# A hybrid encoder layer: the attention loop by pairs of steps

## The chip, the cores and the metric

The kernel runs on one core of one Trainium2 chip. The metric is the time of one execution on the device in microseconds; the median of three runs counts. The core has five engines with a queue each, which run side by side and wait for each other by semaphores: TensorE (PE; its weight loads are shown apart as PEld), VectorE (DVE), ScalarE (ACT), GpSimd (POOL) and SyncE (SP, which issues most transfers). On each of them instructions start in the order in which the program lists them.

## The reference

One layer of a Hymba-style encoder: 2048 positions, width 1024, float32. A normed input is projected once; its columns feed an attention branch (MLA, 4 heads) and a state-space branch (S5, 32 groups of channels, forward and backward); both are normed, gated, concatenated, projected and added to the input.

```python
h = _rms_norm(x, pre_norm_g[l]);  z = h @ w_in[l]
z_q, z_kv, z_kr, g_attn, u_ssm, g_ssm = jnp.split(z, split_points, axis=-1)
...
def attend_block(args):                         # 128 queries, all 4 heads, all 2048 keys
    qn, qr = args
    s = (jnp.einsum('bqhd,bkhd->bhqk', qn, k_nope, preferred_element_type=jnp.float32)
         + jnp.einsum('bqhr,bkr->bhqk', qr, k_rope, preferred_element_type=jnp.float32))
    p = jax.nn.softmax(s * scale, axis=-1).astype(v.dtype)
    return jnp.einsum('bhqk,bkhd->bqhd', p, v)
...
ssm = _s5_bidirectional(u_ssm, ...)             # two associative scans over the positions
ssm = jax.nn.gelu(ssm);  ssm = ssm * jax.nn.sigmoid(ssm @ w_glu[l] + b_glu[l])
mixed = jnp.concatenate([attn, ssm], axis=-1) @ w_out[l]
x = x + _rms_norm(mixed, post_norm_g[l])
```

## The kernel before

Three phases. Phase 1 (to about 390 us) computes `z` in tiles of 128 positions. Phase 3 (from about 1200 us) gates both branches and multiplies by `w_out`. The change lies in phase 2 between them: one loop in which attention and S5 are interleaved by hand. No scheduler reorders it (`manual_schedule`): each engine gets its instructions in the order in which the code emits them, and a wait is put wherever an instruction needs another engine's result or a buffer that is still in use.

Products are made in float32r with operands split in a high and a low part (`hi + lo`). A **unit** is one head of one block of 256 queries (two query tiles of 128); there are 32 units (`NU`), of 8 **steps** each, 256 steps in all. Step `t` of unit `n` does the following (`i = t % 8`):

- `scores` (L1098): five matmuls of 128 queries against 512 keys into the PSUM tile `sc` (pool `psS`, 2 buffers), then on VectorE `nm`, the row maximum of these 512 scores (L1108).
- `transp` (L1145): four transposes by TensorE, of an older step's normed exponentials, into the PSUM tile `pt` (pool `psP`, 2 buffers). ScalarE copies it to `phi`, the high part (L1159); VectorE later makes `plo`, the low part, as `pt - phi` (L1573). Both lie in pool `pp`, 2 buffers each.
- `expo` (L1111): ScalarE makes `e = exp(sc - max)` with its row sum (L1114).
- `stats` (L1118), once per unit: VectorE and ScalarE work out the factors `f` that bring the four blocks of a row to one maximum and divide by the sum; `norm` (L1135) multiplies an `e` by its factor, on ScalarE (L1143) for most of the loop, on VectorE (L1139) in its last 23 steps.
- `av` (L1163): six matmuls of `phi` and `plo` with the keys' compressed values into `av`. After the eighth of a unit ScalarE copies it to `avs` (L1176), and `unit_out` multiplies by the head's value weights (`po`).

The lags, in steps behind the scores: `norm` 9 (`NLAG`), `transp` 11 (`LAG`), `av` 12 (`LAG + AVLAG`). So TensorE's order in a step is five matmuls of scores, four transposes, six of `av` for the transposes of the step before.

Between these stand the steps of S5 (`s5_pre`, `s5_post`): a group of channels starts every 7 steps (`START`; two of them 6 steps apart) and takes 15. On VectorE a group needs `ta`, `tb` (L996, L997), `X` (L1001), four scans (L1008, L1009), `hc` twice (L1017, L1021) and a split `wTl` (L196), nearly all in `s5_pre`, ahead of a step's `nm`. GpSimd makes `tb2` (L1018) and the tables of the next groups (L971, L972, L975). The queries of the next block (`qprep`: matmuls, copies L730 and L761, and on VectorE L732, L746, L764) are made a piece per step at a step's end. In the last 23 steps `out_weights` prepares the weights of phase 3 in the same place, with a copy on ScalarE (L1228) in each step.

Of the kernel before, what the change touches and what calls it, by code (L numbers as in the profile page):

```python
# [147 lines left out]
def tile_hymba(ctx, tc, x, pos, inv_freq, pre_g, w_in, q_g, w_uqT, w_uqr, kv_g, w_ukT, w_uv, attn_g,  # L148
# [202 lines left out]
    def s5_params():  # L351
# [37 lines left out]
        # F = (lam_bar - 1) / lam  # L389
# [17 lines left out]
        # powers of lam_bar, 0 .. T, in the order of each direction  # L407
# [29 lines left out]
        # phasors of chunk 32 i + 2 j + a: ph32 * (0..7) (+ phi), for a = 0, 1, and ph2 * (0..15)  # L437
# [13 lines left out]
        for nm, src in (("b", ph2), ("a", ph32)):  # L451
# [21 lines left out]
            # the backward direction turns the other way  # L473
# [11 lines left out]
        # B_bar = F B; B'' = B_bar e^{-i phi}; C' = lam_bar C  # L485
# [3 lines left out]
        def cm(orr, oi, ar, ai, xr_, xi_):  # L489
            """(orr, oi) = (ar + i ai)(xr + i xi), a over the last dimension."""  # L490
# [32 lines left out]
        # centre lag: Re(C B_bar) of both directions + D  # L523
        # (eight groups at a time: theirs are the blocks on the diagonal)
# [36 lines left out]
    def step():  # L561
        """A slice of the tables, of about BUDGET elements."""
# [15 lines left out]
    # absorbed weights: W_uq[h] W_uk[h]^T  # L578
# [23 lines left out]
    # the first tile is loaded and normed by halves  # L602
# [48 lines left out]
    # ------------------------------------------------------------------ phase 2  # L651
    # (the gate columns of the last two tiles run under its start)
# [5 lines left out]
    ep = pool(ph2, "ep", 13)  # L658
# [37 lines left out]
    # queries of a block of 256: each piece's last results are split a step later  # L696
# [74 lines left out]
    def both(*gens):  # L771
        """Step some routines in turn; what each returns."""
# [14 lines left out]
    # the gate columns of the last two tiles run under the start of the attention  # L787
# [58 lines left out]
    # S5  # L846
# [8 lines left out]
    def s5_load(q):  # L855
        """The tables of four groups."""
# [34 lines left out]
    def ops4(tile_, q_r, q_i, c1, c2):  # L891
        """The operands of tile_[., 2, s, h] = q_r[s] c1[., h] + q_i[s] c2[., h]."""
# [9 lines left out]
    def two(eng, tile_, tmp, *o):  # L902
        """The two products of a table; later they are added."""
# [18 lines left out]
    def k_build(q):  # L922
        """The kernels of the lags within a chunk, and their windows for each position."""
# [755 lines left out]
```

## Time and profile before

| | us |
|---|---|
| three runs: median (lowest to highest) | 1434.57 (1433.16 to 1434.58) |
| the profiled execution: span, first to last instruction | 1431.5 |
| attention loop: first score to last score | 394.2 to 1169.2 |
| of it with S5 (steps 3 to 228) | 400.5 to 1098.1 |
| of it with the weights of phase 3 (steps 233 to 255) | 1111.3 to 1167.9 |

The page gives no time of its own for the profiled execution beside its span, which is 3.1 us below the median of the runs. Busy time of an engine is the time in which at least one of its instructions ran; on TensorE these overlap, and their ends are modelled. A row of a timeline gives start, duration, engine, line, what is written and read, and in brackets how long the engine had stood idle and what released it.

### The profile page before, as it was taken

What the parts mean: (1) busy time and instruction counts of PE and PEld (TensorE: products, weight loads), DVE (VectorE), ACT (ScalarE), POOL (GpSimd) and SP (SyncE); (2) the same over time, 40 slices, a digit from 0 to 9 for tenths busy, and PEclk for the clock granted to TensorE, in tenths of its full rate; (3) what the DMA queues carried; (4) which work ended last, traced back from release to release, by engine and by line L of the source; (5) the groups of instructions that cost most, each with busy time, mean ns of one, the idle gap of its engine ahead of it and who ended that gap; (6) DMA issues with size and microseconds to landing.
All of it is one profiled execution on the core that took longest, in us unless ns stands there. A gap on an engine that the chain in (4) does not pass through costs nothing.

```text
span 1431.5 us, 24291 instructions
## 1 busy us (share of the span) xinstructions
PE 1359.6 (95%) x9016; PEld 1221.6 (85%) x9016; DVE 1053.7 (74%) x1876; ACT 789.0 (55%) x1796; POOL 624.9 (44%) x616
## 2 busy tenths in 40 slices
PE   7999999999989999999999998999999989999998
PEld 7999999999968788887888887887888878788886
DVE  5456545332588888898989888988888895876774
ACT  6321222122457767767677676676677775544542
POOL 2102321233364655555556555645542695323340
PEclk9999999999999999999999999999999999999999
DMA  8322332442610110201102011020100345345432
GB/s 293 89 61 66 80 87 73 98 122 73 150 35 19 39 34 5 54 19 31 41 5 61 12 32 41 23 43 5 32 5 9 101 128 131 118 148 179 145 103 88
DMA packets 122133, 102.91 MB, mean 72 GB/s; under 512 B 14672, under 2 KB 107104, under 8 KB 122016
## 3 DMA queue, kind: packets, MB, share of 16 engines
q1 hardware_dynamic: 110384, 89.43, 22.3%
q0 software_dynamic: 2272, 7.62, 2.0%
q10 hardware_dynamic: 9360, 4.33, 1.5%
q8 instruction: 70, 1.15, 0.3%
q14 instruction: 47, 0.39, 0.1%
HBM read 63.80 MB, written 37.54 MB: 71 GB/s over the span
## 4 chain that ended last, share of the span: by engine, by line
PE 59%; DVE 26%; ACT 5%; issue 4%; POOL 2%; DMA 2%; SPq 1%; ACTq 0%; POOLq 0%; DVEq 0%
DVE plo L1573 5%; DVE nm L1108 4%; PE po L202 4%; PE po L203 4%; PE po L204 4%; PE pt L1151 3%; DVE hc L1017 3%; DVE G L1009 3%; DVE G L1008 3%; PE z_ga L203 2%; PE z_ga L204 2%; PE z_ga L202 2%; PE av L1173 2%; PE z_u L204 2%; PE z_u L202 2%
## 5 line engine op out<-in xcount | busy, mean ns | idle before, releaser
L1114 ACT ACTIVATE e<-sc,nm 128x512 f32<-128x512 f32 x256 | 176.4, 689 | 141.1 <-DVE nm L1108 139.8
L1573 DVE TENSOR_TENSOR plo<-pt,phi 128x512 fp32r<-128x512 f32 x255 | 175.0, 686 | 49.2 <-ACT phi L1159 46.3
L1159 ACT ACTIVATE phi<-pt 128x512 fp32r<-128x512 f32 x256 | 152.8, 597 | 72.9 <-PE pt L1151 72.4
L1108 DVE TENSOR_REDUCE nm<-sc 128x1 f32<-128x512 f32 x256 | 175.0, 683 | 17.6 <-PE sc L1107 15.6
L1173 PE MATMUL av<-plo,kn_h 128*128 128x256 f32 x512 | 150.6, 294 | 30.0 <-DVE plo L1573 29.5
L1171 PE MATMUL av<-phi,kn_h 128*128 128x256 f32 x512 | 165.7, 324 | 13.3 <-ACT avs L1176 13.2
L1143 ACT ACTIVATE e<-e,f 128x512 f32<-128x512 f32 x226 | 163.8, 725 | 1.5 <-DVE f L1132 1.5
L1151 PEld LDWEIGHTS pt<-ident,e 128*128 128x128 f32 x1024 | 127.8, 141 | 38.9 <-DVE e L1139 4.5
L1151 PE MATMUL pt<-ident,e 128*128 128x128 f32 x1024 | 154.8, 274 | 4.3 <-DVE e L1139 3.5
L1172 PE MATMUL av<-phi,kn_l 128*128 128x256 f32 x512 | 144.6, 282 | 0.0
L1173 PEld LDWEIGHTS av<-plo,kn_h 128*128 128x128 f32 x512 | 96.5, 189 | 40.1 <-DVE plo L1573 39.3
L1018 POOL TENSOR_TENSOR tb<-G,t 128x512 f32<-128x512 f32 x32 | 41.6, 1301 | 192.2 <-DVE G L1009 192.2
L1103 PE MATMUL sc<-kT_h,qo 128*128 128x512 f32 x256 | 114.7, 448 | 2.9 <-ACT e L1114 1.4
L1171 PEld LDWEIGHTS av<-phi,kn_h 128*128 128x128 f32 x512 | 97.6, 191 | 16.6 <-ACT avs L1176 16.5
L202 PE MATMUL po<-woh,ah 128*128 128x512 f32 (+1 forms) x264 | 102.6, 389 | 1.9 <-ACT u L1410 1.9
L203 PE MATMUL po<-wol,ah 128*128 128x512 f32 (+1 forms) x264 | 102.4, 388 | 0.0
L204 PE MATMUL po<-woh,al 128*128 128x512 f32 (+1 forms) x264 | 102.3, 388 | 0.0
L1104 PE MATMUL sc<-kT_l,qo 128*128 128x512 f32 x256 | 101.5, 396 | 0.0
L1106 PE MATMUL sc<-krS,qo 128*128 128x512 f32 x256 | 101.3, 396 | 0.0
L1107 PE MATMUL sc<-krS,qo 128*128 128x512 f32 x256 | 101.2, 395 | 0.0
L1105 PE MATMUL sc<-kT_h,qo 128*128 128x512 f32 x256 | 100.8, 394 | 0.0
L1172 PEld LDWEIGHTS av<-phi,kn_l 128*128 128x128 f32 x512 | 97.7, 191 | 0.0
(337 smaller groups left out, 4148.6 us busy)
## 6 DMA issues: line engine op xcount, KB each, us to landing
g_d<-gst SPq DMA_DIRECT2D x64, 128.0 KB, 2.0
g<-g_d SPq DMA_DIRECT2D x16, 512.0 KB, 5.7
xr<-in_x_dram SPq DMA_DIRECT2D x16, 512.0 KB, 6.7
xt<-in_x_dram SPq DMA_DIRECT2D x15, 512.0 KB, 3.8
out_dram<-res SPq DMA_DIRECT2D x15, 512.0 KB, 3.1
u_d<-ust ACTq DMA_DIRECT2D x64, 64.0 KB, 2.1
u<-u_d SPq DMA_DIRECT2D x64, 64.0 KB, 2.5
o_d<-o SPq DMA_DIRECT2D x32, 128.0 KB, 1.8
```

The lines of the kernel that those rows point to most:

```text
L202: PE.matmul(ps, ahi, bhi, start=first, stop=False)
L203: PE.matmul(ps, ahi, blo, start=False, stop=False)
L204: PE.matmul(ps, alo, bhi, start=False, stop=last)
L1108: V.tensor_reduce(st["nm"][:, qt, kb:kb + 1], ps, AX.X, ALU.max, negate=True)
L1114: A.activation(e, st.pop("s"), AF.Exp, bias=st["nm"][:, qt, kb:kb + 1], accum_out=st["L"][:, qt, kb:kb + 1])
L1143: A.activation(e, e, AF.Copy, scale=f)
L1151: PE.transpose(pt[:, kk, qt, :], st["e"][qt, kt // 4][:, o:o + P], ident)
L1159: A.activation(hi, ptf, AF.Copy)
L1171: PE.matmul(o, kn_h[:, kt, :], hi[:, w], start=kt == 0, stop=False)
L1172: PE.matmul(o, kn_l[:, kt, :], hi[:, w], start=False, stop=False)
L1173: PE.matmul(o, kn_h[:, kt, :], lo[:, w], start=False, stop=kt == NT - 1)
L1573: V.tensor_tensor(lo[0], lo[1], f32(lo[2]), ALU.subtract)
```

## The change

The loop goes by pairs of steps. Pair `p` covers steps `2p` and `2p + 1`:

- `scores` makes two score tiles, of both query tiles with the same 512 keys: ten matmuls, and after each five its `nm`.
- Both `transp` of the pair follow, eight transposes in a row. They only write `pt`; the copies to `phi` and the subtractions for `plo` are now written in the loop, behind both `expo`, the first half of `stats`, the S5 steps `s5_post(2p)` and the piece `between(2p)` of the next queries or weights.
- Then `unit_out`, the first `av`, `s5_pre(2p + 1)`, the second `av`, `s5_post(2p + 1)`, `between(2p + 1)`.
- The lags become 4, 5 and 6 pairs: `norm` 8, `transp` 10, `av` 12 steps behind the scores, two steps at a time. `av` works on the transposes of the pair before.
- Pool `ep` (tiles `e`) has 12 buffers in place of 13; `pp`, `psP` and `psS` keep 2 per tag. A pair writes two `phi` and two `plo` while those of the pair before are still to be read by its `av`.
- The last unit's norms are given out at once, to V, A, V, A, G, G, G, G.

The rest is the same: the instructions and their sizes, phases 1 and 3, S5. Comments and docstrings are gone, which moves line numbers a little (`nm` L1109, `e` L1115, `norm` L1144, `transp` L1152, `av` L1170 to L1172, `phi` L1612, `plo` L1614).

```diff
-    ep = pool(ph2, "ep", 13)
+    ep = pool(ph2, "ep", 12)
...
+    def scores(qo, st, k):
+        c = slice(k * 512, (k + 1) * 512)
+        st["s"] = []
+        for qt in range(2):
+            w = slice(qt * P, (qt + 1) * P)
+            ps = psS.tile([P, 512], F32, tag="s", name="sc")
...
+            V.tensor_reduce(st["nm"][:, qt, k:k + 1], ps, AX.X, ALU.max, negate=True)
+            st["s"].append(ps)
...
-        ptf = pt.rearrange("p a b c -> p (a b c)")
-        A.activation(hi, ptf, AF.Copy)
         st["p"][j] = hi, lo
-        return lo, ptf, hi
+        return pt.rearrange("p a b c -> p (a b c)"), hi, lo
...
-    NLAG, LAG, AVLAG = 9, 11, 1
+    NLAG, LAG, AVLAG = 4, 5, 6
...
-    for t in range(8 * NU + LAG + AVLAG + 3):
...
+    for p in range(4 * NU + AVLAG + 1):
+        n, k = divmod(p, 4)
+        t = 2 * p
...
+        if not tail and p >= NLAG:
+            for i in range(2):
+                m, kk = divmod(p - NLAG, 4)
+                norm(sts[m], 2 * kk + i, "A" if state[0] is None else "V")
...
+        s5_pre(t)
...
+            scores(qo[b][h], sts[n], k)
+        m, kk = divmod(p - LAG, 4)
+        pts = [transp(sts[m], 2 * kk + i, p3) for i in range(2)] if 0 <= m < NU else []
+        if not tail:
+            for i in range(2):
+                expo(sts[n], 2 * k + i)
+            if k == 3:
+                sts[n]["stats"] = stats(sts[n])
+                run(sts[n]["stats"], 1)
+        s5_post(t)
...
+            between(t)
+        for pt_, hi_, lo_ in pts:
+            A.activation(hi_, pt_, AF.Copy)
+        for pt_, hi_, lo_ in pts:
+            V.tensor_tensor(lo_, pt_, f32(hi_), ALU.subtract)
...
+            unit_out(*units[m], sts.pop(m))
+        m, kk = divmod(p - AVLAG, 4)
+        if 0 <= m < NU:
+            av(sts[m], 2 * kk)
+        s5_pre(t + 1)
+        if 0 <= m < NU:
+            av(sts[m], 2 * kk + 1)
+        s5_post(t + 1)
...
+            between(t + 1)
```

What this does to the order on two engines, each at the same place of the program: around the four scans of one S5 group and the end of a unit, where `m` and `f` of `stats` stand. Names are those of the code; the numbers behind `pt`, `G`, `X` are buffers. ScalarE before, three steps:

```order
L1143 ACTIVATE e<-e,f 128x512
L887 ACTIVATE mh<-m_8026 128x512
L1159 ACTIVATE phi<-pt_8218 128x512
L1114 ACTIVATE e,L<-sc,nm 128x512
L1037 ACTIVATE y_2_7421<-py 128x2x128
L1143 ACTIVATE e<-e,f 128x512
L1159 ACTIVATE phi<-pt_8260 128x512
L1114 ACTIVATE e,L<-sc,nm 128x512
L1125 ACTIVATE f<-f 128x8
```

ScalarE in the changed kernel, two pairs:

```order
L1144 ACTIVATE e<-e,f 128x512 x2
L1115 ACTIVATE e,L<-sc,nm 128x512 x2
L1037 ACTIVATE y_3_8523<-py 128x2x128
L1612 ACTIVATE phi<-pt_8790 128x512
L1612 ACTIVATE phi<-pt_8797 128x512
L1181 ACTIVATE o<-po 128x256
L730 ACTIVATE qo_1_8838<-psq,kvgs 128x256
L1144 ACTIVATE e<-e,f 128x512 x2
L1115 ACTIVATE e,L<-sc,nm 128x512 x2
L1126 ACTIVATE f<-f 128x8
L1612 ACTIVATE phi<-pt_8871 128x512
L1612 ACTIVATE phi<-pt_8878 128x512
```

`phi` stood ahead of its step's `e`; now both `phi` stand behind both `e`, and behind what `s5_post`, `between` and `stats` put there (`y`, `f`). VectorE before, two steps:

```order
L1108 TENSOR_REDUCE nm<-sc 128x1
L1573 TENSOR_TENSOR plo<-pt_8218,phi 128x512
L1008 SCALAR_TENSOR_TENSOR G_4637<-tab_6803,X_4639 64x255
L1009 SCALAR_TENSOR_TENSOR G_4637<-tab_6803,X_4639 64x255
L1008 SCALAR_TENSOR_TENSOR G_4637<-tab_6803,X_4639 64x255
L1009 SCALAR_TENSOR_TENSOR G_4637<-tab_6803,X_4639 64x255
L1108 TENSOR_REDUCE nm<-sc 128x1
L1122 TENSOR_REDUCE m<-nm 128x2
L1124 TENSOR_TENSOR f<-m,nm 128x8
L1573 TENSOR_TENSOR plo<-pt_8260,phi 128x512
```

VectorE in the changed kernel, from one pair's second `plo` to the next pair's:

```order
L1614 TENSOR_TENSOR plo<-pt_8797,phi 128x512
L1008 SCALAR_TENSOR_TENSOR G_4637<-tab_6831,X_4639 64x255
L1009 SCALAR_TENSOR_TENSOR G_4637<-tab_6831,X_4639 64x255
L1008 SCALAR_TENSOR_TENSOR G_4637<-tab_6831,X_4639 64x255
L1009 SCALAR_TENSOR_TENSOR G_4637<-tab_6831,X_4639 64x255
L1017 TENSOR_TENSOR hc<-G_4637,t_8596 128x512
L1109 TENSOR_REDUCE nm<-sc 128x1 x2
L1123 TENSOR_REDUCE m<-nm 128x2
L1125 TENSOR_TENSOR f<-m,nm 128x8
L732 SCALAR_TENSOR_TENSOR qo_1_8838<-psq,kvgs,qo_1_8838 128x256
L1614 TENSOR_TENSOR plo<-pt_8871,phi 128x512
L1614 TENSOR_TENSOR plo<-pt_8878,phi 128x512
```

One `nm` and one `plo` took turns, with S5 between the steps; now two `nm` come, then what `s5_post(2p)`, `between(2p)` and `stats` have (here `m`, `f`, `qo`), two `plo`, and then the S5 work of both steps together. TensorE's order is ten matmuls of scores, eight transposes, and twelve of `av` with the S5 and query products between.

## Rows read from the trace of the kernel before

**Rows 1.** Page, part 1: busy us, share of the span, instructions.

```profile
PE 1359.6 (95%) x9016; PEld 1221.6 (85%) x9016; DVE 1053.7 (74%) x1876; ACT 789.0 (55%) x1796; POOL 624.9 (44%) x616
```

**Rows 2.** Windows: start:end, us, each engine's busy us, granted clock, DMA.

```profile
400.48:1098.09 697.61, 653.12 (x4270) 571.04 (x4269) 616.44 (x1053) 489.25 (x1150) 383.87 (x360) 1.00 0.11 26
...
1111.29:1167.93 56.64, 53.78 (x339) 46.45 (x338) 47.87 (x80) 40.76 (x94) 42.78 (x36) 1.00 0.39 110
```

**Rows 3.** Waits in 400.48 to 1098.09, by engine: us, times, longest.

```profile
PE av L1173 <- DVE plo L1573: 28.3, 32, 2.6
PE av L1171 <- ACT avs L1176: 12.8, 11, 1.8
...
DVE plo L1573 <- ACT phi L1159: 34.1, 70, 1.4
...
ACT e L1114 <- DVE nm L1108: 133.3, 109, 3.9
```

**Rows 4.** Timeline, ScalarE and VectorE in steps 103 to 105.

```profile
701.25 0.60 ACT L1159 ACTIVATE phi<-pt 128x512 fp32r<-128x512 f32 x1 [0.89 <-PE pt L1151]
...
701.88 0.69 DVE L1573 TENSOR_TENSOR plo<-pt,phi 128x512 fp32r<-128x512 f32 x1 [0.32 <-ACT phi L1159]
...
708.02 0.69 DVE L1108 TENSOR_REDUCE nm<-sc 128x1 f32<-128x512 f32 x1
...
708.75 0.69 ACT L1114 ACTIVATE e<-sc,nm 128x512 f32<-128x512 f32 x1 [0.28 <-DVE nm L1108]
...
709.43 0.71 ACT L1143 ACTIVATE e<-e,f 128x512 f32<-128x512 f32 x1
```

**Rows 5.** Timeline, TensorE: the first score matmul of two steps without S5.

```profile
1165.62 0.40 PE L1103 MATMUL sc<-kT_h,qo 128*128 128x512 f32 x1
...
1167.92 0.40 PE L1103 MATMUL sc<-kT_h,qo 128*128 128x512 f32 x1
```

**Rows 6.** Groups in 400.48 to 1098.09: count, busy us, mean ns, idle before.

```profile
L196 DVE TENSOR_TENSOR wTl<-pw,wTh 128x256 fp32r<-128x256 f32 x32 | 13.6, 425 | 15.6 <-ACT wTh L195 15.5
L732 DVE SCALAR_TENSOR_TENSOR qo<-psq,kvgs,qo 128x256 fp32r<-128x256 f32 x28 | 13.2, 473 | 0.0
...
L764 DVE TENSOR_TENSOR qo<-ptr,qo 128x128 fp32r<-128x128 f32 x56 | 12.2, 278 | 0.0
...
L1124 DVE TENSOR_TENSOR f<-m,nm 128x8 f32<-128x8 f32 x28 | 8.6, 308 | 1.0
...
L730 ACT ACTIVATE qo<-psq,kvgs 128x256 fp32r<-128x256 f32 x28 | 13.1, 469 | 3.5 <-PE psq L204 3.5
L195 ACT ACTIVATE wTh<-pw 128x256 fp32r<-128x256 f32 x32 | 12.3, 384 | 0.0
L1037 ACT ACTIVATE y<-py 128x256 f32<-128x256 f32 x31 | 11.8, 382 | 3.6 <-PE py L1034 3.6
L761 ACT ACTIVATE qo<-ptr 128x128 fp32r<-128x128 f32 x56 | 10.8, 283 | 1.6 <-PE ptr L758 1.6
...
L1125 ACT ACTIVATE f<-f 128x8 f32<-128x8 f32 x28 | 5.7, 205 | 0.2 <-DVE f L1124 0.2
```

**Rows 7.** Groups in 1111.29 to 1167.93: the weights' copy.

```profile
L1228 ACT ACTIVATE woh<-raw,ga 128x512 fp32r<-128x512 f32 x15 | 10.8, 721 | 5.3 <-DMA raw<-in_w_out_dram 5.3
```

**Rows 8.** S5's `hc`: its two groups (400.48 to 1098.09), then single ones.

```profile
L1017 DVE TENSOR_TENSOR hc<-G,t 128x512 f32<-128x512 f32 x32 | 52.3, 1635 | 0.0
...
L1021 DVE TENSOR_TENSOR hc<-hc,tb 128x512 f32<-128x512 f32 x31 | 40.7, 1311 | 2.5 <-POOL tb L1018 2.5
...
621.48 2.02 DVE L1017 TENSOR_TENSOR hc<-G,t 128x512 f32<-128x512 f32 x1
...
710.02 0.68 DVE L1017 TENSOR_TENSOR hc<-G,t 128x512 f32<-128x512 f32 x1
```

**Rows 9.** Windows around the longest wait of TensorE; the clock comes after POOL.

```profile
510.00:515.00 5.00, 2.40 (x13) 1.93 (x12) 4.78 (x10) 1.97 (x5) 4.37 (x4) 0.89 0.15 25
515.00:520.00 5.00, 4.92 (x27) 4.05 (x26) 4.75 (x9) 3.30 (x8) 2.44 (x3) 0.77 0.00 0
```

More of the change, by code (lines that the diff above doesn't have):

```diff
@@ L1545, in tile_hymba, with between @@
     p3 = None
-    TAIL = [[(0, "V"), (1, "A"), (2, "G"), (3, "G")], [(k, "G") for k in range(4, 8)]]
-    for t in range(8 * NU + LAG + AVLAG + 3):
+    TAIL = "VAVAGGGG"
+    def between(t):
         n, i = divmod(t, 8)
-        if n >= 1 and i == 0 and n - 1 < NU:
-            run(sts[n - 1]["stats"], 1)
-        if t < 8 * NU and t >= NLAG:
-            norm(sts[(t - NLAG) // 8], (t - NLAG) % 8, "A" if late is None else "V")
-        s5_pre(t)
+        late_, qb_, qn_ = state
         if n < NU:
@@ L1557, in tile_hymba @@
             b, h = units[n]
-            if i == 0:
+            if b + 1 < 8:
+                k = 8 * h + i
+                if k == 0:
+                    qb_, qn_ = qprep(b + 1, psQ, "q"), 0
+                held = qn_ % 2 == 1
+                if qb_ and (held if i == 3 else i != 4 and PLACE.get(t, (0, 0))[1] in QOFF):
+                    qn_ += 1
+                    try:
+                        next(qb_)
+                    except StopIteration as e_:
+                        qo[b + 1] = e_.value
+                        qb_ = None
@@ new lines, in between @@
+            if h == NH - 1 and i == 7:
+                assert b == 7 or b + 1 in qo
+                qo.pop(b)
+            if late_ is None and t >= START[NG] + 8 and b == 7:
+                s5x.close()
+                ph2q.close()
+                late_ = out_weights()
+        if late_ is not None:
+            next(late_, None)
+        state[:] = late_, qb_, qn_
+    state = [None, None, 0]
+    for p in range(4 * NU + AVLAG + 1):
+        n, k = divmod(p, 4)
+        t = 2 * p
+        tail = n >= NU
+        if k == 0 and n >= 1 and n - 1 < NU:
+            run(sts[n - 1]["stats"], 1)
+        if not tail and p >= NLAG:
+            for i in range(2):
+                m, kk = divmod(p - NLAG, 4)
+                norm(sts[m], 2 * kk + i, "A" if state[0] is None else "V")
+        elif p == 4 * NU:
+            for i, eng in enumerate(TAIL):
+                norm(sts[NU - 1], i, eng)
+        s5_pre(t)
+        if not tail:
+            b, h = units[n]
+            if k == 0:
@@ L1601, in tile_hymba @@
-        if n < NU and h == NH - 1 and i == 7:
-            assert b == 7 or b + 1 in qo
-            qo.pop(b)
-        if late is None and t >= START[NG] + 8 and b == 7:
-            s5x.close()
-            ph2q.close()
-            late = out_weights()
-        if late is not None:
-            next(late, None)
-        if t == 8 * NU - 1:
-            assert next(late, "end") == "end"
+        s5_post(t)
+        if tail:
+            next(p3)
+        else:
+            between(t)
+        for pt_, hi_, lo_ in pts:
+            A.activation(hi_, pt_, AF.Copy)
@@ new lines, in tile_hymba @@
+        for pt_, hi_, lo_ in pts:
+            V.tensor_tensor(lo_, pt_, f32(hi_), ALU.subtract)
+        m, kk = divmod(p - AVLAG - 1, 4)
+        if 0 <= m < NU and kk == 3:
+            unit_out(*units[m], sts.pop(m))
+        m, kk = divmod(p - AVLAG, 4)
[5 more added lines that the diff above has]
+        s5_post(t + 1)
+        if tail:
+            next(p3)
+        else:
+            between(t + 1)
@@ L1612, in tile_hymba @@
+        if p == 4 * NU - 1:
+            assert next(state[0], "end") == "end"
             ph3w.close()
```

59 lines of the change are left out of this document (8 added, 51 removed).

## The prediction

> **What bounds the kernel now.** I read the page's first part, the windows of the attention loop, the waits inside it, and then a few steps of its timeline. The page shows TensorE busy for 95% of the span [rows 1], so one looks for its waits first. The loop has to be read by itself. While S5 runs beside attention (steps 3 to 228, 697.6 us), VectorE is busy for 616.4 us, ScalarE for 489.3 and GpSimd for 383.9 [rows 2]: two engines are nearly full there. TensorE's waits are few: 28.3 us in 32 waits for `plo`, 12.8 us in 11 waits for `avs` [rows 3]. They come where S5's burst on VectorE (scans, `hc`) delays a step's `plo`, which `av` wants one step later. VectorE idles for 697.6 - 616.4 = 81.2 us, of which 34.1 us are waits for `phi` [rows 2, 3].
>
> So the loop is bound by TensorE with VectorE close behind, and the question is not only what the change takes from TensorE's 41 us of waits, but what it asks of VectorE. VectorE has a slack of 81.2 us. Of the 112.5 pairs of this stretch 109 hold transposes (the first ones come in pair 5), so that is 0.74 us for each of these.
>
> **What the change does to TensorE.** The matmuls are the same in number and size. A plain step starts 2.30 us after the one before [rows 5], a plain pair takes 4.6 us, and with S5 and queries TensorE is busy for 653.1 / 112.5 = 5.8 us a pair [rows 2]. Eight transposes in a row in place of twice four change a wait for a weight load at most; no row shows eight here, TensorE does not set the pace below, and I cost it at nothing. `av` follows its transposes by a pair, behind ten score matmuls and eight transposes, so `plo` and `avs` get about two more microseconds than in the step-wise order. The two waits of [rows 3] lose their cause: up to 41 us, if TensorE stays the bound.
>
> **What it does to ScalarE and VectorE.** This is the term that I think decides. Before, ScalarE's order in a step is `phi`, then `e`: `phi` waits only for the transposes, so VectorE can go from `nm` to `plo` almost at once. In the timeline one `plo` starts 0.04 us behind its `nm`, at 708.75 [rows 4]. In the changed order both `e` stand ahead of both `phi` on ScalarE, and on VectorE both `nm` ahead of both `plo`, with the S5 work behind them. As each engine keeps its order, every pair now runs through one chain: second `nm` (VectorE), second `e`, first `phi` (ScalarE), first `plo` (VectorE), second `plo`, S5, next pair's `nm`. From the end of the second `nm` to the start of the first `plo` VectorE can only do what the code puts between. The parts of that gap are in [rows 4]: `nm` ends at 708.71 and `e` starts at 708.75 (0.04); ScalarE takes its next instruction at 709.43 (0.68); a `phi` takes 0.60; `plo` starts at 701.88, 0.03 behind the `phi` that began at 701.25. That is 1.35 us, and it is larger than the 0.74 us of slack.
>
> What fills the gap on VectorE: `f` of `stats` always (8.6 us in all), and for even steps alone `wTl`, `qo` twice, half of (13.6 + 13.2 + 12.2) us [rows 6]. Together 28.1 us. What lengthens it on ScalarE, by standing ahead of `phi`: the exponential of `f` (5.7 us), and half of `wTh`, `y` and the two `qo` copies, half of (12.3 + 11.8 + 13.1 + 10.8) us [rows 6]. Together 29.7 us. These cancel but for 1.6 us; smaller groups of both kinds are left out.
>
> The sum for this stretch: VectorE's own work 616.4, plus 109 x 1.35 = 147.2, plus 1.6, is 765.2 us against 697.6 now: **+68 us**. TensorE's 5.8 us a pair then lies within the chain's 6.8, and the removed waits come back as waits for the chain.
>
> **The last 22 steps** (233 to 254, 11 pairs, 56.6 us with VectorE busy for 47.9 [rows 2]). Here the norms are on VectorE, and each `between` puts a copy of weights on ScalarE, 0.72 us [rows 7]; that of the even step now stands in the gap. 47.9 + 11 x (1.35 + 0.72) = 70.7 us: **+14 us**. The steps between both stretches and the loop's first steps have little VectorE work; I take them as they are. Behind the last scores the transposes and `av` go on without `e`, so the chain is absent; the norms of the last unit are spread in another way, worth some 2 us either way.
>
> **The unknown price: S5's `hc`.** Its two instructions take 1.64 and 1.31 us in the mean, single ones 0.68, others 2.02 [rows 8]; by the timeline the long ones run beside GpSimd's work on the next tables. The change moves both in time against GpSimd. All 64 short would give 32 x (0.96 + 0.63) = 51 us back, all long would cost 32 x (0.38 + 0.71) = 35 us. GpSimd's order is the same and it still starts that work when the scans end, so I take the means as they are and keep both ends for the range. [...]
>
> Sum: 1431.5 + 68 + 14 = 1513.5 us of span; the runs' median lies 3.1 us above the profiled span, so **1517 us**, 5.7% slower.
>
> **Rivals.**
>
> *The chain is covered and TensorE keeps the pace (faster).* If VectorE's forced idle time were below 0.74 us a pair, the loop would not be longer than now; below 5.8 - 616.4 / 112.5 = 0.33 us TensorE alone would set it, and its 41 us of waits would go: about 1394 us. For it speaks that these waits are plain in [rows 3] and that `av` gets a pair's time. Against it: ScalarE already waits 133.3 us for `nm` [rows 3], so `e` follows VectorE closely, and the order leaves VectorE nothing else to do. 6 in 100. That the idle time comes out near 0.74 us, as more work falls into the gap than I counted: 1435 us, 4 in 100.
>
> *TensorE's side of the pair joins the chain (slower still).* `pp` keeps two buffers, so a pair's `phi` must wait until the same pair's `av` has read the older `phi`, and `av` stands behind the transposes and what S5 and the queries put there. Two S5 groups span seven pairs; in the three of them with least S5 work on VectorE the `av` may end later than the second `e`, by up to a microsecond. 109 x 3/7 x 1.0 = 47 us: about 1564 us. For it: TensorE needs 5.8 us a pair and the chain 6.8, a small margin. Against: in the other pairs the chain is the longer by far. 7 in 100.
>
> *The clock falls.* [...] 8 in 100.
>
> **How the numbers follow.** The forecast gets 75 in 100, the rivals 6, 4, 7 and 8. The range takes in most of the `hc` ends and of the two slower rivals: 1517 - 47 = 1470 to 1562 us. About 0.2% (3 us) is what a measurement of this kernel can tell from no change; so faster 0.06, the same 0.04, slower 0.90.
>
> **What would show it.** Right: `plo` waits for `phi` on VectorE some 100 times, by 1.0 to 1.4 us each, far over 100 us in sum against 34.1 now; `av` no longer waits for `plo` or `avs`; TensorE's waits move to `pt` for `plo` and to `sc` for `e`; VectorE's busy time stays near 616 us in a stretch of about 765. Wrong: if TensorE's waits shrink and the stretch is under 697 us, the chain is covered; if TensorE shows long stretches at the lower clock, or `phi` waits for `av` rather than for its place behind `e`, one of the slower rivals holds; if `hc` moves by more than 20 us in sum, the price of [rows 8] was the mistake.

## The result, and the profile after

The changed kernel takes **1537.5 us** (median of 4 runs, 1536.4 to 1538.0) against 1434.4 us: the ratio is 1.072, 95% interval 1.0704 to 1.0735. The forecast was 1517 us in a range of 1470 to 1562: the direction and the mechanism held, the size was 20 us short. The profiled execution spans 1534.7 us against 1431.5, so 103.1 us are to be found in the trace.

Of these, 85.3 us lie in steps 3 to 228 (782.9 us against 697.6, [rows 2]), 14.5 in steps 234 to 254 (66.4 against 51.8 us), and the remaining 3.3 before, between and behind these (5.2 more from step 254 to the end, 271.1 against 265.9 us, and 2 less ahead of step 3). The windows of these two stretches in the changed kernel (start:end, us, busy us of PE, PEld, DVE, ACT and POOL, granted clock, DMA):

```profile
398.44:1181.37 782.93, 682.64 (x4279) 595.65 (x4277) 592.78 (x1056) 485.26 (x1151) 384.87 (x362) 0.96 0.11 24
1197.19:1263.56 66.37, 54.48 (x309) 44.72 (x307) 47.66 (x75) 35.35 (x83) 40.48 (x34) 0.95 0.33 91
```

VectorE was 88% busy in the S5 stretch and is now 76% busy (592.8 of 782.9 us). No engine is full: the loop is set by engines that wait for each other. The same stretch by waits (us, times, longest):

```profile
ACT e L1115 <- DVE nm L1109: 180.8, 101, 4.9
DVE plo L1614 <- ACT phi L1612: 110.3, 75, 3.2
...
PE sc L1104 <- ACT e L1115: 64.0, 35, 3.7
...
DVE plo L1614 <- PE av L1171: 30.7, 17, 3.6
DVE nm L1109 <- PE sc L1108: 18.9, 21, 3.2
DVE wTl L196 <- ACT wTh L195: 18.6, 17, 1.7
ACT phi L1612 <- PE av L1171: 11.9, 18, 1.5
...
PE ptr L758 <- ACT o L1181: 10.2, 7, 3.5
PE psq L202 <- ACT o L1181: 9.4, 5, 3.2
```

`av` no longer waits for `plo` or `avs`, whose 28.3 and 12.8 us stood first in [rows 3]. In their place TensorE waits 64.0 us for `e` ahead of its scores and 23.1 us for `o` ahead of the query products (`ptr`, `psq` and 3.5 us of `psr`), and VectorE 110.3 + 30.7 us ahead of `plo`. The groups of VectorE in that stretch (count, busy us, mean ns, idle time before them):

```profile
L1614 DVE TENSOR_TENSOR plo<-pt,phi 128x512 fp32r<-128x512 f32 x216 | 141.7, 688 | 142.6 <-ACT phi L1612 110.3 <-PE av L1171 30.7
...
L1021 DVE TENSOR_TENSOR hc<-hc,tb 128x512 f32<-128x512 f32 x31 | 39.9, 1288 | 0.6
L1017 DVE TENSOR_TENSOR hc<-G,t 128x512 f32<-128x512 f32 x31 | 30.7, 989 | 0.4
...
L196 DVE TENSOR_TENSOR wTl<-pw,wTh 128x256 fp32r<-128x256 f32 x32 | 13.4, 418 | 18.6 <-ACT wTh L195 18.6
```

`plo` and the `wTl` that lies ahead of it in even steps collect 142.6 + 18.6 = 161.2 us of idle time. The chain of waits through one such pair, in which the exponential of `f` (0.20 us) stands between `e` and `phi` (start, us, what):

```profile
716.58 0.61 DVE nm L1109
...
717.21 1.31 ACT e L1115 x3
...
718.91 0.61 ACT phi L1612
...
720.16 0.68 DVE plo L1614
```

This is the forecast chain: `nm`, `e`, `phi`, `plo` hand the work from VectorE to ScalarE and back, one after the other.

A second path was not forecast. The timeline of one place, TensorE, ScalarE and VectorE (start, us; in brackets the idle time before it and what ended that), and the window of the scores that follow:

```profile
660.00 0.38 PE L202 MATMUL psq<-zh,wab_h 128*128 128x256 f32 x1 [2.19 <-ACT o L1181]
```

```profile
658.59 1.09 ACT L1612 ACTIVATE phi<-pt 128x512 fp32r<-128x512 f32 x2
659.54 0.41 ACT L1181 ACTIVATE o<-po 128x256 f32<-128x256 f32 x1
```

```profile
662.95 0.69 DVE L1109 TENSOR_REDUCE nm<-sc 128x1 f32<-128x512 f32 x1 [2.44 <-PE sc L1108]
664.90 0.69 DVE L1109 TENSOR_REDUCE nm<-sc 128x1 f32<-128x512 f32 x1 [1.26 <-PE sc L1108]
```

```profile
661.30:664.70 3.40, 3.40 (x10) 2.53 (x9) 0.69 (x1) 2.19 (x5) 0.00 (x0) 0.53 0.02 5
```

`o`, the copy of a unit's output out of the one PSUM buffer that it shares with the query products, stands on ScalarE behind both `e` and both `phi`. The query product waits 2.19 us for it; in the 3.40 us of the window behind that wait the granted clock is 0.53 in the mean, while TensorE is busy throughout, and both `nm` of the next pair wait, 3.7 us in sum.

### The profile page after: what moved, and what is told of

The parts are those of the page before. It is cut to its first block, busy times and chain, and to the rows that moved or that the text cites. A ratio compares the mean times of both kernels' runs of the same rounds, so it can differ in the third digit from the quotient of the medians.

```text
span 1534.7 us, 24449 instructions
## 1 busy us (share of the span) xinstructions
PE 1396.6 (91%) x9016; PEld 1250.6 (81%) x9016; DVE 1033.1 (67%) x1876; ACT 783.3 (51%) x1798; POOL 620.0 (40%) x614
## 4 chain that ended last, share of the span: by engine, by line
PE 59%; DVE 22%; ACT 11%; issue 6%; DMA 2%; SPq 1%; POOL 0%; ACTq 0%; DVEq 0%; POOLq 0%
ACT e L1115 5%; DVE plo L1614 4%; PE pt L1152 3%; PE po L202 3%; PE po L203 3%; PE po L204 3%; DVE nm L1109 3%; ACT phi L1612 3%; PE sc L1104 3%; DVE G L1009 2%; DVE G L1008 2%; PE sc L1105 2%; PE sc L1106 2%; PE sc L1107 2%; PE sc L1108 2%
## 5 line engine op out<-in xcount | busy, mean ns | idle before, releaser
L1614 DVE TENSOR_TENSOR plo<-pt,phi 128x512 fp32r<-128x512 f32 x256 | 167.6, 688 | 171.8 <-ACT phi L1612 136.1
L1115 ACT ACTIVATE e<-sc,nm 128x512 f32<-128x512 f32 x256 | 173.8, 682 | 213.7 <-DVE nm L1109 213.4
L1144 ACT ACTIVATE e<-e,f 128x512 f32<-128x512 f32 x228 | 153.9, 736 | 83.8 <-DVE f L1133 83.8
L1104 PE MATMUL sc<-kT_h,qo 128*128 128x512 f32 x256 | 115.4, 451 | 78.6 <-ACT e L1115 77.0
L1109 DVE TENSOR_REDUCE nm<-sc 128x1 f32<-128x512 f32 x256 | 165.9, 682 | 20.7 <-PE sc L1108 19.4
L1170 PE MATMUL av<-phi,kn_h 128*128 128x256 f32 x512 | 158.9, 310 | 0.0
L1612 ACT ACTIVATE phi<-pt 128x512 fp32r<-128x512 f32 x256 | 142.1, 602 | 15.2 <-PE av L1171 11.9
L1152 PEld LDWEIGHTS pt<-ident,e 128*128 128x128 f32 x1024 | 121.2, 144 | 31.0 <-DVE plo L1614 15.3
L1172 PE MATMUL av<-plo,kn_h 128*128 128x256 f32 x512 | 145.4, 284 | 0.0
L1152 PE MATMUL pt<-ident,e 128*128 128x128 f32 x1024 | 139.9, 278 | 5.9 <-DVE plo L1614 5.6
L1104 PEld LDWEIGHTS sc<-kT_h,qo 128*128 128x128 f32 x256 | 51.2, 200 | 97.7 <-ACT e L1115 87.8
L1106 PE MATMUL sc<-kT_h,qo 128*128 128x512 f32 x256 | 107.0, 418 | 0.0
L1107 PE MATMUL sc<-krS,qo 128*128 128x512 f32 x256 | 107.0, 418 | 0.0
L1108 PE MATMUL sc<-krS,qo 128*128 128x512 f32 x256 | 106.0, 414 | 0.0
L1170 PEld LDWEIGHTS av<-phi,kn_h 128*128 128x128 f32 x512 | 98.7, 193 | 1.1
```

Source lines behind the costliest of these rows:

```text
L1104: PE.matmul(ps, qo[:, 0, w], kT_h[:, c], start=True, stop=False)
L1109: V.tensor_reduce(st["nm"][:, qt, k:k + 1], ps, AX.X, ALU.max, negate=True)
L1115: A.activation(e, st["s"][qt], AF.Exp, bias=st["nm"][:, qt, kb:kb + 1], accum_out=st["L"][:, qt, kb:kb + 1])
L1144: A.activation(e, e, AF.Copy, scale=f)
L1152: PE.transpose(pt[:, kk, qt, :], st["e"][qt, kt // 4][:, o:o + P], ident)
L1170: PE.matmul(o, kn_h[:, kt, :], hi[:, w], start=kt == 0, stop=False)
```

## The experiments

All compute the whole result. Stage times are from the first score matmul of step 4 to that of step 228 ("S5 stretch", one step less than in [rows 2]) and of step 234 to 254 ("late"). They come from the profiled execution, which lies within 0.3% of the median, for e10 0.7% above it. Each ratio is against runs of the kernel before that were made beside it.

| kernel | median us | ratio to before | S5 stretch | late |
|---|---|---|---|---|
| before | 1434.4 | 1 | 696.5 | 51.8 |
| changed | 1537.5 | 1.072 | 780.0 | 66.4 |
| e1 `plo` behind S5 | 1469.4 | 1.026 | 709.2 | 67.3 |
| e2 three buffers | 1525.6 | 1.065 | 770.0 | 67.8 |
| e3 `e, phi, e, phi` | 1529.9 | 1.067 | 782.4 | 59.9 |
| e4 before, `phi` behind `e` | 1611.1 | 1.124 | 859.2 | 63.4 |
| e5 norms behind | 1544.6 | 1.078 | 803.9 | 54.0 |
| e6 `phi` ahead of `e` | 1472.2 | 1.026 | 730.5 | 56.9 |
| e7 `phi`, `plo` at the end | 1557.9 | 1.087 | 800.2 | 62.3 |
| e8 before, lag of two | 1453.1 | 1.014 | 717.7 | 50.9 |
| e9 e1, e2, e6 together | 1503.9 | 1.049 | 747.8 | 58.1 |
| e10 e9, norms ahead of `e` | 1636.4 | 1.144 | 887.9 | 57.9 |
| e11 before, e8's buffers | 1434.3 | 1.001 | 694.8 | 52.3 |
| e12 e1, e2, late norms | 1453.1 | 1.015 | 702.7 | 55.0 |

**e4: the chain alone, in the kernel before.**

```
-        A.activation(hi, ptf, AF.Copy)
...
         if n < NU:
             expo(sts[n], i)
+        if lo is not None:
+            A.activation(lo[2], lo[1], AF.Copy)
+        if n < NU:
...
```

> The kernel before, step by step as it was, with phi moved behind e on ScalarE and nothing else. It puts the chain nm, e, phi, plo into every step without any pair of steps. Theory A: 217 steps x 1.35 us = 293 us of idle time on VectorE, of which its 81 us of slack and some 30 us of f and query work take a part, and 22 late steps x 1.35 = 30 us: 1434 + 180 to 240, so 1615 to 1675 us. Rival C (the order of e and phi matters little; what costs is the pair itself: two nm and ten scores at once against two score buffers, the lag, the slow clock): under 1480 us.

Measured: 1611.1 us, ratio 1.124 (1.1228 to 1.1261), 179 us slower than the kernel before beside it. A wait of its S5 stretch, and two of its steps on VectorE (the wait is in brackets):

```profile
DVE plo L1575 <- ACT phi L1566: 274.3, 216, 1.4
```

```profile
705.31 0.69 DVE L1575 TENSOR_TENSOR plo<-pt,phi 128x512 fp32r<-128x512 f32 x1 [1.34 <-ACT phi L1566]
705.92 0.68 DVE L1108 TENSOR_REDUCE nm<-sc 128x1 f32<-128x512 f32 x1
707.93 0.69 DVE L1575 TENSOR_TENSOR plo<-pt,phi 128x512 fp32r<-128x512 f32 x1 [1.33 <-ACT phi L1566]
```

The line taken out is that of `transp`, which is called ahead of `expo`. No pair is formed and no lag is changed, and each `plo` waits 274.3 / 216 = 1.27 us: 1.33 where nothing lies between, the 1.35 us of the prediction to within 0.02. Theory A's price of the chain is right; rival C (the pair itself, not the order of `e` and `phi`) would have left this kernel under 1480 us. The whole is 4 us below the expected 1615 to 1675; VectorE's own work, which that range had taken as fixed, was 42 us shorter (last section).

**e1: S5 work put into the gap.**

```
-        for pt_, hi_, lo_ in pts:
-            V.tensor_tensor(lo_, pt_, f32(hi_), ALU.subtract)
...
             between(t + 1)
+        for pt_, hi_, lo_ in pts:
+            V.tensor_tensor(lo_, pt_, f32(hi_), ALU.subtract)
```

> The changed kernel, with both plo subtractions written at the end of the pair, so that VectorE does the pair's S5 and query work between the second nm and the first plo; nothing else moves. Theory A (forced idle time of VectorE sets the pair): in the changed kernel VectorE sits idle for 161.6 us in 108 pairs between the second nm and the first plo, and the work that now stands behind plo covers 139.5 us of that, pair by pair. TensorE's own work (653 us in this stretch before) then stops the gain: 1537 - 115 to 127, so 1410 to 1422 us, up to 1450 where S5 waits for something else. Rival B (TensorE's side of the pair, phi and plo waiting for av, or the slow clock, carries most of the loss): plo comes later, phi stays, so at most 40 us are won: 1497 us or more.

Measured: 1469.4 us, ratio 1.026 (1.024 to 1.0274): 68 us of the 103 come back by moving the two `plo` on one engine, far more than rival B's 40. But the time lies in neither range: it is 47 to 59 us above A's forecast, and 19 above the 1450 that A allowed where S5 waits for something else. The group of `plo`, then the waits and the window of its S5 stretch:

```profile
L1628 DVE TENSOR_TENSOR plo<-pt,phi 128x512 fp32r<-128x512 f32 x216 | 141.0, 685 | 19.3 <-ACT phi L1612 13.0 <-PE av L1171 4.6
```

```profile
DVE wTl L196 <- ACT wTh L195: 36.3, 30, 2.5
DVE nm L1109 <- PE sc L1108: 26.5, 33, 3.3
...
DVE qo L732 <- ACT qo L730: 10.4, 10, 2.4
```

```profile
401.27:1110.49 709.22, 658.77 (x4267) 574.15 (x4267) 595.01 (x1051) 489.02 (x1149) 385.72 (x359) 0.99 0.11 26
```

`plo`'s idle time fell by 123.3 us (142.6 to 19.3). Some 44 us of that turned up elsewhere: `wTl` now waits 17.7 us more, `qo`, `ta` and `nm` together 26 more, because S5's own instructions wait for ScalarE and TensorE when they are reached earlier. Work moved into a gap covers it only so far as it is ready. The late steps, which have no S5 work, did not move (67.3 us).

**e2: a third buffer for `phi` and `plo`.**

```
-    pp = pool(ph2, "pp", 2)
-    op = pool(ph2, "op", 2)
+    pp = pool(ph2, "pp", 3)
+    op = pool(ph2, "op", 1)
```

> The changed kernel with three buffers each for phi and plo in place of two (one buffer each for avs and o pays for the space), so that a pair's first phi no longer waits for av of the pair before. Theory A: 18 pairs have phi waiting for av, 11.9 us in sum; the rest of the chain stays: 5 to 25 us less, 1512 to 1532 us. Rival B (two buffers are what closes the chain): the 42.6 us of waits for av (30.7 on VectorE, 11.9 on ScalarE) go, and the slow clock that follows TensorE's waits with them: 1495 us or less.

Measured: 1525.6 us, ratio 1.065 (1.0635 to 1.0667), 12 us under the changed kernel and within theory A's range. `plo` no longer waits for `av`, but its waits for `phi` grow from 110.3 to 130.8 us, so 10 of the 141.0 are gone. The query products wait for `o` as long as before (`ptr` 9.8, `psq` 9.7 us against 10.2 and 9.4), so the single buffer of `o` that pays for this shows no cost there. The rival of the two buffers was real and small.

**e3: the first `phi` ahead of the second `e`.**

```
+        for i in range(2):
+            if not tail:
+                expo(sts[n], 2 * k + i)
+            if pts:
+                A.activation(pts[i][1], pts[i][0], AF.Copy)
         if not tail:
-            for i in range(2):
-                expo(sts[n], 2 * k + i)
...
-        for pt_, hi_, lo_ in pts:
-            A.activation(hi_, pt_, AF.Copy)
```

> The changed kernel with ScalarE's order e, phi, e, phi in place of e, e, phi, phi; VectorE's order stays. Theory A: the first phi no longer waits for the second e, so the idle time ahead of plo falls from 1.41 us to about 0.70 in a plain pair: 108 x 0.7 = 76 us less, 1461 us, give or take 20. Rival B: phi, now earlier, meets the av that still reads its buffer, and the second e waits behind it: no gain, 1530 us or more.

Measured: 1529.9 us, ratio 1.067 (1.0638 to 1.0709); 8 us, not 76. The late steps gain 6.5 us (59.9 against 66.4) and the work behind the last scores 3.3; the S5 stretch gains nothing (782.4 against 780.0). Its group of `plo` and two of its waits:

```profile
L1615 DVE TENSOR_TENSOR plo<-pt,phi 128x512 fp32r<-128x512 f32 x216 | 147.1, 689 | 123.4 <-ACT phi L1604 106.3 <-PE av L1171 15.6 <-PE av L1172 0.7
```

```profile
ACT phi L1604 <- PE av L1171: 41.8, 32, 3.3
DVE wTl L196 <- ACT wTh L195: 36.4, 17, 2.8
```

The first `plo` starts earlier, but the second now waits for a `phi` that stands behind the second `e`, and S5 stands behind both. The time ahead of both `plo` and of `wTl` is 123.4 + 36.4 = 159.8 us, nearly the 161.2 of the changed kernel. `phi` also waits 41.8 us for `av` where it waited 11.9, as rival B said. My expectation had looked at one link: as long as VectorE makes both `plo` ahead of the S5 work, the gap lasts until both `e` and both `phi` are done, and this order does not shorten that.

**e6: both `phi` ahead of both `e`.**

```
...
+        for pt_, hi_, lo_ in pts:
+            A.activation(hi_, pt_, AF.Copy)
         if not tail:
             for i in range(2):
                 expo(sts[n], 2 * k + i)
...
-        for pt_, hi_, lo_ in pts:
-            A.activation(hi_, pt_, AF.Copy)
```

> The changed kernel with both phi ahead of both e on ScalarE, as the kernel before has it, and the three buffers of e2 (so that the first phi has not to wait for av). Pairs, score order, lag and VectorE's order stay. Theory A (the order of e and phi is what costs): plo no longer waits for e; of e2's 130.8 us of waits for phi a third or less is left, and 1526 falls by 70 to 110 us: 1416 to 1456 us. Rival D (the pair itself costs: ten scores against two score buffers, so that TensorE waits for e whichever way ScalarE's order is): TensorE's waits for e (59 us in e2) stay or grow, since e now stands behind phi: 1490 us or more.

Measured: 1472.2 us, ratio 1.026 (1.0242 to 1.0276), 53 us under e2, whose buffers it has. Between A and D: the order of `e` and `phi` is half of the 103 us, and the rest stays. Two of its waits:

```profile
ACT phi L1601 <- PE av L1171: 83.6, 91, 2.2
...
PE sc L1104 <- ACT e L1115: 43.3, 59, 3.1
```

`phi` now waits for `av` 91 times, in spite of three buffers, since the second `phi` of a pair still writes where the pair before is being read; both `e` stand behind it, and TensorE still waits 43.3 us for `e` (58.9 in e2). From these waits I read a ring without VectorE: TensorE (scores, transposes, `av`), then ScalarE (`phi`, `e`), then the next scores. No run gives `phi` and `plo` four buffers, which would test it directly.

**e5: the norms behind `phi`.**

```
-        if not tail and p >= NLAG:
-            for i in range(2):
-                m, kk = divmod(p - NLAG, 4)
-                norm(sts[m], 2 * kk + i, "A" if state[0] is None else "V")
-        elif p == 4 * NU:
+        late0 = state[0] is None
+        if p == 4 * NU:
...
             scores(qo[b][h], sts[n], k)
+        if not tail and p >= NLAG and state[0] is not None:
+            for i in range(2):
+                m_, k_ = divmod(p - NLAG, 4)
+                norm(sts[m_], 2 * k_ + i, "V")
...
             A.activation(hi_, pt_, AF.Copy)
+        if not tail and p >= NLAG and late0:
+            for i in range(2):
+                m_, k_ = divmod(p - NLAG, 4)
+                norm(sts[m_], 2 * k_ + i, "A")
```

> The changed kernel with the pair's two norms moved: behind both phi on ScalarE, and in the last 22 steps behind both nm on VectorE. Nothing else moves. In one pair of four the norms wait for f, which VectorE makes behind all the S5 work of the pair before (80.3 us of ScalarE's waits, 28 times), and both e stand behind the norms. Theory A with this second chain: the 27 pairs lose up to two norms of 0.68 us from the way to phi, 18 to 37 us, and in the late steps the norms fill the idle time ahead of plo, 11 x 1.3 = 14 us: 1537 - 32 to 51, so 1486 to 1505 us. Rival (f and the norms are hidden, as e waits for nm anyway): only the late steps gain, 1520 us or more.

Measured: 1544.6 us, ratio 1.078 (1.0752 to 1.0802). The late steps gained 12.4 us, as expected; the S5 stretch lost 24. Waits of its S5 stretch:

```profile
DVE nm L1109 <- PE sc L1108: 41.7, 34, 4.3
...
PE ptr L758 <- ACT o L1181: 21.1, 7, 4.9
...
PE psq L202 <- ACT o L1181: 16.4, 6, 3.5
...
PE psr L202 <- ACT o L1181: 7.3, 4, 2.2
```

The wait of the norms for `f` (80.3 us in the changed kernel) is gone from the list and `plo`'s idle time is the same (141.9 against 142.6 us): it had been hidden, as the rival said. Most of what was added is on the path through `o`: it now stands behind the norms as well, the query products wait 44.8 us for it in place of 23.1, and `nm` waits 41.7 us for scores in place of 18.9. The transposes also wait for the norms now, 9.5 us.

**e7: both at the pair's end**, with the norms ahead of them.

```
-        for pt_, hi_, lo_ in pts:
-            A.activation(hi_, pt_, AF.Copy)
-        for pt_, hi_, lo_ in pts:
-            V.tensor_tensor(lo_, pt_, f32(hi_), ALU.subtract)
...
             between(t + 1)
+        for pt_, hi_, lo_ in pts:
+            A.activation(hi_, pt_, AF.Copy)
+        for pt_, hi_, lo_ in pts:
+            V.tensor_tensor(lo_, pt_, f32(hi_), ALU.subtract)
```

> The changed kernel with both phi and both plo at the end of the pair, behind all its S5 and query work on ScalarE and VectorE, and with the norms moved as in e5. Theory A: in e1 36 us of waits of wTl for wTh and 59 us of norms for f were left; VectorE's idle time goes on falling, and TensorE sets the pace: its 653 us in the S5 stretch against 709 in e1 is 30 to 55 us under e1's 1469, so 1415 to 1440 us. Rival D (two score buffers for a pair of scores): TensorE's waits for e and VectorE's for the scores (14 and 26 us in e1) grow by what the others give back: 1455 us or more.

Measured: 1557.9 us, ratio 1.087 (1.0852 to 1.0885). Theory A missed it; rival D's open range (1455 us or more) holds it, but not by D's cause alone: TensorE's waits for `e` grow from 14.3 to 36.9 us, while `nm` waits 4.8 us for scores in place of 26.5. Two other waits of its S5 stretch:

```profile
DVE plo L1633 <- ACT phi L1631: 129.6, 86, 4.4
...
PE pt L1152 <- DVE plo L1633: 48.2, 49, 1.9
```

`phi` is now behind ScalarE's copies of S5 and query products, and these come from the end of TensorE's pair; `plo` waits for `phi` again, and the next transposes for `plo`. Its norms are moved too, so not all of the 88 us over e1 is this.

**e8 and e11: the lag alone, in the kernel before.**

```
-    ep = pool(ph2, "ep", 13)
-    pp = pool(ph2, "pp", 2)
-    op = pool(ph2, "op", 2)
+    ep = pool(ph2, "ep", 12)
+    pp = pool(ph2, "pp", 3)
+    op = pool(ph2, "op", 1)
...
-    NLAG, LAG, AVLAG = 9, 11, 1
+    NLAG, LAG, AVLAG = 9, 11, 2
...
-        lag = AVLAG + (t >= 8 * NU)
+        lag = AVLAG
...
```

e11 has the first six lines alone. The last change, with two more lines of its kind, is for the steps behind the last scores, where `av` had a lag of two already; what follows the last scores takes as long as before (265.9 us in both).

> The kernel before, in single steps, with av two steps behind its transposes in place of one (three buffers each for phi and plo; one each for avs and o, and 12 for e, pay for the space). It is the part of the change that could gain, alone. Theory A: the 41 us of TensorE's waits for plo and avs lose their cause and VectorE's 81 us of idle time leave room, so 25 to 41 us go: 1392 to 1408 us. Rival E (the burst of S5 on VectorE holds back pt and the scores instead, as the transposes wait for plo in the two buffers of pt): the waits move to pt and sc, under 10 us are won: 1423 us or more.

> The kernel before with the buffers of e8 alone (three for phi and plo, one for avs and o, 12 for e), av one step behind as it was. It tells how much of e8's 19 us is the lag. If the lag did it: within 3 us of the kernel before, 1431 to 1437 us. If the scarcer buffers did it: 1445 us or more.

Measured: e8 1453.1 us, ratio 1.014 (1.0119 to 1.0152); e11, the buffers without the lag, 1434.3 us, 1.001 (0.9996 to 1.002). So the lag alone makes the kernel before slower. Waits of e8's S5 stretch, and its window:

```profile
PE sc L1103 <- ACT e L1114: 23.0, 26, 2.9
...
PE av L1171 <- ACT avs L1176: 16.1, 13, 2.2
...
PE ptr L758 <- ACT o L1182: 6.4, 5, 1.9
```

```profile
399.72:1117.40 717.68, 661.58 (x4258) 574.74 (x4258) 610.73 (x1049) 490.40 (x1147) 383.12 (x359) 0.98 0.11 26
```

`av`'s 28.3 us for `plo` are gone, as the change means it; those for `avs` are not (16.1 us, 12.8 before). And S5's burst on VectorE is still there: TensorE runs on and then waits for `e` ahead of the scores (23.0 us, 1.4 before), and as `unit_out` moves with the lag, the query products wait for `o` (6.4 us at `ptr`, 5.7 at `psq`), which they had not. TensorE idles 717.7 - 661.6 = 56.1 us in place of 696.5 - 652.0 = 44.5, and is busy 9.6 us longer with the same matmuls, at a granted clock of 0.98: together the 21 us that the stretch has grown by. A had called for a gain. E's range (1423 us or more) holds the result; of the two places that E named for the wait, `sc` got it and `pt` did not.

**e9, e10 and e12: the cures together.** e9 has e1's `plo`, e2's buffers, e6's `phi`, and the late norms behind `nm`. e10 moves ScalarE's norms from ahead of `phi` to between `phi` and `e`. e12 is e9 with ScalarE's order as in the changed kernel.

```
 # ScalarE, one pair
 e9:   norm norm phi phi e e
 e10:  phi phi norm norm e e
 e12:  norm norm e e ... phi phi
```

> The changed kernel with the cures of e1, e2 and e6 together: both phi ahead of both e on ScalarE, both plo behind the pair's S5 and query work on VectorE, three buffers for phi and plo; in the last 22 steps the norms on VectorE stand behind nm (the part of e5 that gained). Theory A: what e1 has left (709 us in the S5 stretch, with 13 us of plo waiting for phi and 14 of phi for av) goes towards TensorE's 655 to 660 us, to about 690, and the late steps to 55 us: 1434 - 6 + 3 + 4 for the end = 1435 us, 1425 to 1448. Rival D (ten scores against two score buffers make TensorE and VectorE wait in turn): 709 us or more stays, and the sum is 1452 us or more.

> As e9, with ScalarE's norms between phi and e in place of ahead of phi, so that the wait of one pair in four for f (57 us in e6) does not hold back phi. Theory A: 0 to 20 us under e9, as phi is what plo and av wait for. If instead e is what TensorE waits for (rival D), the norms stand ahead of e in both and nothing changes: within 5 us of e9.

> The changed kernel with e1's plo behind S5, e2's three buffers, and in the last 22 steps VectorE's norms behind nm; ScalarE's order (e, e, phi, phi) stays. If the gains add where no order of ScalarE is touched: e1's 1469, less some 10 us for the 13.8 us of phi waiting for av, less 12 us in the late steps: 1440 to 1455 us. If two cures get in each other's way as in e9: 1465 us or more. Faster than the kernel before (1433) only if TensorE's other waits go as well, which nothing here does.

Measured: e9 1503.9 us (1.0471 to 1.0518), e10 1636.4 us (1.1396 to 1.1479), e12 1453.1 us (1.0118 to 1.0175). e12 came out as expected. e9 lies in rival D's range and is worse than either of its halves, and e10 fell outside both of its expectations by 127 us or more. A piece of e10's chain of waits:

```profile
717.15 1.01 PE pt L1152 x8
...
719.26 0.60 ACT phi L1602
719.86 1.22 ACT e L1144 x2
721.08 1.34 ACT e L1115 x4
...
722.75 0.66 PE ptr L758 x4
723.40 0.24 PE sc L1104
```

Here the ring of e6 is closed: transposes and `av`, `phi`, the norms (1.22 us), `e`, and then TensorE's next products. Two norms more between `phi` and `e` cost 132 us between the medians, 1.2 us for each of 109 pairs, the same as their duration here. So the two norms between the transposes and `e` were paid in full. In e9 `phi` is on this ring and S5's copies, which VectorE needs ahead of `plo`, stand behind it: its `wTl` waits 52.3 us for `wTh` and its `qo` 30.4, against 36.3 and 10.4 in e1. I take that for the reason that e9 loses what e1 gained; no run tested it alone.

None of these beats the kernel before. The best, e12, is 19 us behind it: 6.2 in the S5 stretch, 3.2 in the late steps, and some 10 behind the last scores, where `plo` now stands behind the work of the next phase (e1 has these too, e2 not).

## Why the prediction was right, and where it was short

**The chain.** Right. In the kernel before, `plo` could start as soon as its `nm` had ended (at 708.71, [rows 4]), since its `phi` had ended at 708.47:

```profile
708.75 0.69 DVE L1573 TENSOR_TENSOR plo<-pt,phi 128x512 fp32r<-128x512 f32 x1
```

The hand-over was forecast at 1.35 us a pair, and e4 shows 1.33 us by itself. Idle time for it was put at 147.2 + 1.6 = 148.8 us; it is 161.2, and e2 explains 10 of the 12 us between: pairs in which `phi` waits for `av`. That this idle time sets the pace is shown by e4, which makes it without pairs, and by e1 and e6, which take part of it away.

**VectorE's own work.** It was carried over at 616.4 us and came out at 592.8. `hc` took 30.7 + 39.9 = 70.6 us (62 of them) against 93.0 (63) in [rows 8], so 22.4 us of the 23.7 are the term that the prediction had left at its mean, with 51 us as the lower end. It had read the long `hc` as those beside GpSimd's work; the last section shows that it turns on which of the two starts first (0.68 us for an `hc` that finds no GpSimd instruction running, otherwise an end some 0.55 us behind that instruction), and the order of the pair decides that.

**What the sum left out.** It took VectorE as idle only for the chain. There were 782.9 - 592.8 - 161.2 = 28.9 us of other idle time on VectorE, 18.9 of it `nm` waiting for scores. By the timeline some 14 us of these follow a wait of TensorE for `o`, as in the place shown above. In other pairs it is TensorE's own work that comes last: ahead of the pair of 716 us the chain of waits runs over scores, transposes and `av` from 706.98 to 712.4 and reaches `phi` at 712.61. Together: 765.2 - 23.7 + 12.4 + 28.9 = 782.8 us against 782.9 measured; this is a bookkeeping of VectorE's time and must close. The step that fell short is the one that let TensorE's 5.8 us a pair lie within the chain's 6.8: it does in the mean, but `o` was not looked at when ScalarE's order was read, and with it and the two buffers TensorE is late in some pairs. Two errors, -24 and +41, partly cancelled, so that the sum came out as near as it did is in part luck.

**The removed waits.** The prediction gave them 41 us "if TensorE stays the bound", and priced a rival at 1394 us by it. e8 shows that this gain was not there even without the pair: the lag leaves the wait for `avs`, moves the one for `plo` to the scores and the query products, and costs 19 us. The rival was given 6 in 100, but its price was wrong as well.

**The late steps.** +14 us were forecast for 11 pairs, and 10 pairs took 14.5 more. e5 and e12 show that these are the gap too: with the norms of VectorE put into it, 12.4 us (e5) and 11.4 us (e12) come back. From step 254 on it takes 5.2 us more, where the prediction had allowed some 2.

**The slower rivals.** Two buffers: priced at 47 us, worth 12 (e2). The clock: in the S5 stretch it was granted at 0.96 in the mean against 1.00 in [rows 2], so that by an estimate from these (1.00 - 0.96) x 782.9 = 31 us of full clock were lost, and the same matmuls kept TensorE busy for 682.6 us in place of 653.1. How much of it lies on the path was not settled: no run here changes the clock alone, so none shows by itself what a falling clock, which got 8 in 100 and a share in the upper end of the range, costs. In e1, whose TensorE idles for 709.2 - 658.8 = 50.4 us of the stretch in place of 782.9 - 682.6 = 100.3, it is 0.99.

**Signs that were named.** `plo` waited for `phi` 75 times, 110.3 us in sum, 1.47 us each in the mean, near the 100 times and 1.0 to 1.4 us that were forecast; 17 more waits (30.7 us) ended with `av`, which is the two buffers' rival. TensorE's waits went to the scores for `e`; those of the transposes for `plo` that I also named did not come. VectorE's busy time did not stay near 616 us, and `hc` moved by 22.4 us: by the sign that was named for it, over 20 us, the price of [rows 8] was a mistake.

## What to carry to other kernels

Where engines keep their order, read a reordering as a chain: count what each engine must have finished between an instruction's input and its output, on every engine that the loop goes round, and take as slack only the idle time of the engine that waits. Grouping steps by two doubles each link (here `e`: 1.31 us for two from 717.21, 0.69 for one in [rows 4]) while the buffers between the engines stay the same, and every copy behind the link (here `o`, for which TensorE waits 23.1 us) is late as well; cures of single links (e1 1469.4 us, e6 1472.2) need not add up (e9 1503.9). And a wait that is removed at one place is a gain only if the next place that needs the same late result has slack (e8: 28.3 us gone at `av`, 23.0 in place of 1.4 at the scores).

## What the runs showed of the hardware that I had not expected

VectorE's busy time for the same instructions is not fixed: from step 4 to step 228 it is 615.7 us in the kernel before, 589.9 in the changed one, and 573.3 in e4, with 1050, 1050 and 1051 instructions. The window of e4's S5 stretch:

```profile
400.38:1259.54 859.16, 736.89 (x4265) 607.85 (x4264) 573.34 (x1051) 484.20 (x1147) 380.85 (x359) 0.95 0.09 21
```

Most of the difference between the first two is `hc`: 93.0 us in the kernel before, 70.6 in the changed one; how much of e4's 42.4 us it is, is not shown here. Beside the long `hc` of [rows 8], which took 2.02 us from 621.48, GpSimd ran the first of these rows; the other two are from the changed kernel:

```profile
621.46 1.50 POOL L971 TENSOR_TENSOR t<-tab 128x768 f32<-128x768 f32 x1
```

```profile
724.83 0.68 DVE L1017 TENSOR_TENSOR hc<-G,t 128x512 f32<-128x512 f32 x1
```

```profile
724.84 2.01 POOL L971 TENSOR_TENSOR t<-tab 128x768 f32<-128x768 f32 x1
```

The `hc` that starts 0.02 us behind GpSimd's instruction ends 0.54 us after that has ended; the one that starts 0.01 us ahead of it takes 0.68 us, and GpSimd's instruction 2.01 in place of 1.50. So it goes throughout the S5 stretch of these two kernels: of their 125 `hc`, by the start and end of each in the traces, 124 either found no GpSimd instruction running and took 0.68 us, or ended some 0.55 us behind the one that ran (0.54 to 0.58, and up to 0.66 where an `hc` took its 0.68 us all the same). Work of GpSimd beside it is not enough to make an `hc` long; the row of 0.68 us at 710.02 in [rows 8] had it too, from 710.18, but had started ahead of it. In the kernel before 28 of 32 first `hc` (L1017) found GpSimd running, in the changed kernel 18 of 31, since there `hc` follows the last scan at once in 10 cases. How long the rest of GpSimd's instruction lasts then depends on the order of everything else, so a part of the added wait can be given back in this way; it is no rule, for e10 waits more than e4 and its VectorE is busy for 587.2 us.

The window of e4 shows the reverse for TensorE: 736.9 us of busy time for matmuls that took 652.0 in the kernel before, at a granted clock of 0.95. By an estimate from that clock, (1.00 - 0.95) x 859 = 43, it accounts for about half of these 85 us; no run here separates the rest.
